# A hybrid encoder layer on one core: order of the input products changed, queries and keys kept as fp16 pairs

## The chip, the cores and the metric

The kernel runs on one core of one Trainium2 chip. The metric is device time in microseconds (us), from three runs: 2857.59 us is the median, 2854.87 to 2858.28 the spread. A kernel is a fixed list of instructions for each engine: TensorE (PE in the profile, with its weight loads, PEld), VectorE (DVE), ScalarE (ACT), GpSimd (POOL) and SyncE (SP), which here only issues transfers. Each engine works through its own list in order and waits, instruction by instruction, for semaphores that the others set.

## What is computed

One encoder layer over 2048 tokens of 1024 features, in fp32. Cut to what matters here:

```python
y = rmsnorm(x, norm_mix_g) @ w_in                  # 1024 -> q 512, k 512, v 512, a 512, g 512
q, k = partial_rotary(q), partial_rotary(k)        # 8 heads of 64; 16 of the 64 dimensions turned
att = dilated_sliding_attention(q, k, v)           # windows (128, 1), (512, 4), (2048, 16)
conv = silu(layernorm(depthwise31(a * sigmoid(g)) + conv_b))
h = x + concat([att, conv]) @ w_out
h = h + cross_attention(rmsnorm(h), rmsnorm(mem))  # 256 memory rows, 4 heads
h = h + square(relu(rmsnorm(h) @ w_up)) @ w_down   # 1024 -> 4096 -> 1024
return rmsnorm(h, norm_final_g)
```

The attention runs over three patterns. A pattern (window, d) looks only at tokens that are a multiple of d apart, within half a window. Each gives an output and a log of its softmax denominator, and the three outputs are combined with the softmax of these logs. For d = 16 the 2048 tokens fall into 16 residue classes of 128 tokens, and one head has 16 score blocks of 128 by 128.

## The kernel before

**Products.** fp32 accuracy is got from pairs: a value is held as a high part and a low part (the value minus the high part), and a product of two pairs is three matmuls into one PSUM accumulation: high by high, high by low, low by high (`mm3`, L254). For the products with `w_in` both factors are fp16 pairs. Weights are first multiplied by a power of two: `wscale` (L189) takes the sum of squares of a weight tile on ACT, adds it over the partitions with a one-column matmul into PSUM bank 7 (kind `c`), and computes the factor `sc` and its inverse `e`, which carries one of the four factors in `back`. `scaled_split` (L210) then scales on ACT, rounds to fp16 on ACT, and subtracts on POOL.

**Stages in time.** First, to 150 us, the memory projections and the preparation of x for tokens 0 to 1023. `xprep(n)` (L379) loads 512 tokens in eight tiles `xn` of 256 KB, normalizes them, transposes them on TensorE (tile `xt`), stores the transposed x to DRAM (`xscr`, needed later as residual) and writes the fp16 pair `xh`, `xl`. Then come the products with `w_in`:

- a gated unit, `glu(c, ns)` (L575), for one of four chunks of 128 channels: products with the weights of g and then of a, each for the groups of 512 tokens in `ns`, tanh on ACT, gate on DVE, store to `uscr`. `early01` is groups 0 and 1. Groups 2 and 3 are done during far attention.
- a unit of queries or keys, `lin_qk(isq, c)` (L691), for the four groups of 512 tokens. c is "r" for the rotary dimensions of all heads (with rotary factors loaded, and sums on DVE and POOL), or 0 to 2 for the others. High and low parts are written by ACT and DVE; they are stored to DRAM, for the near patterns in order of tokens (`qscr`), and by residue class for d = 16 (`qfar` for queries; `kscr` for keys, which all patterns use). In DRAM they are fp32 values (type F32R, for TensorE), the high part rounded to that type.
- the values, `lin_v` (L634): the four column blocks of the weights are scaled by `vmul` (from `vscale`, L607, which uses bank 7 four times), and a first matmul takes x as the stationary factor; 16 tiles `v_0` to `v_15` of 128 tokens, stored to `vtok`.

`pipeline` (L555) takes a list of such units as Python generators and runs them one after another, with later units started ahead by some steps (load, scale, split). `weave` (L93) runs a main generator and calls side generators at given rates; `pinned` (L83) marks each step as not to be issued ahead of the latest instruction noted in `last`. From these calls a list scheduler makes the order of every engine.

Beside the products of queries, keys and values runs the depthwise convolution of tokens 0 to 511 (`conv_units`, tile `cacc`, 31 DVE instructions of 128x512 a chunk): two chunks in the pool `conv0` beside the queries and keys, two in `conv0b` beside gated units and values. Both the units and these pools have their order in the main block:

```python
units = list(chain(glu(0, early01), glu(1, early01)))
units += [lin_qk(isq, c) for c in ("r", 0, 1, 2) for isq in (False, True)]
steps = pipeline(*units, *glu(2, early01), *glu(3, early01), lin_v())
...
    weave(islice(steps, 7), (later, 2.5))
...
    weave(islice(steps, 31), (vsc, 0.42), (conv0, 0.58))
```

`later` is the preparation of x for tokens 1024 to 2047.

**Far attention** (540 to 750 us) is the pattern d = 16 for all heads, together with the near patterns d = 4 and d = 1 of tokens 0 to 511, woven with the gated units of tokens 1024 to 2047 (`rest`). `far_keys` (L928) loads one head's keys `k3` as 16 runs of 144 values in a partition, high parts in partitions 0 to 63, low parts in 64 to 127; `far_q` (L933) loads the queries, the high part twice, the low part once into a tile whose other half is zero. So two matmuls over 128 partitions make one score block: the first gives high by high plus high by low, the second low by high. In `att_far` (L941) four blocks make a unit: each score matmul takes one query block against two neighbouring key blocks at once, 256 columns, of which one half is used; four blocks of 256 columns fill two PSUM tiles `s`. Mask and row minimum on DVE and the exponential on ACT (`att_probs`, L874), four transposes on TensorE to `pt`, the pair `ph` on ACT and `pl` on DVE (`att_turn`, L880), and the products with v (`att_pv`, L891) follow, each a step later. Results go to DRAM (`oscr`) and come back in `combine` (L988) as the tile `ld`.

**Passage and dense part.** From 750 to 796 us far attention ends and the first residual tiles `res` and the attention's output `cath` are loaded. From there to 2867 us the output projection, cross attention and MLP run for each group of 512 tokens (`post`), with near attention of the following groups woven in. There the score matmuls of 256 columns are those of L1097; `load_keys` and `keys_of` (L903, L908) load 16 runs of 64 keys and the queries, and `turned` (L921) reorders queries on POOL.

## Time and profile before

| what | value | how to read it |
|---|---|---|
| median of 3 runs | 2857.59 us | the metric |
| the profiled execution's own time | 2868.5 us | one execution, with the profiler |
| its span | 2866.7 us | first to last instruction, in the trace |
| mean granted clock of TensorE | 0.981 | share of full speed that the throttle allowed |
| DRAM read, written | 389, 160 MB | 192 GB/s over the span |
| depthwise convolution on DVE | 480 instructions, 393.1 us | the largest group of DVE |
| mask and minimum on DVE, exponential on ACT | 384 each, 129.1 and 161.8 us | the largest groups of attention |
| mean of an MLP matmul | 390 to 401 ns | matmuls overlap; two starts are less far apart than this |

The profile says how long each engine was busy in a stretch of time, which granted clock TensorE had there, and ahead of every instruction how long its engine had stood idle and what it waited for (in brackets: the idle time in us, an arrow, the engine or transfer that came last). Idle time matters only on the engine that the others wait for. A matmul's duration in the trace is longer than the step to the next, because matmuls overlap: a price per matmul is read from the distance between two starts. In the stretch of far attention PE was busy 166.8 of 191 us.

### The profile page before, as it was taken

The numbers are of one execution on the slowest core, as the hardware profiler recorded it, in microseconds if no ns is written. First come the engines' busy times: TensorE is split into PE (matmuls) and PEld (weight loads), VectorE is DVE, ScalarE is ACT, GpSimd is POOL, SyncE is SP. The second block draws the span as 40 slices with busy tenths as digits, with TensorE's granted clock in tenths as the row PEclk, the third lists the DMA queues.
The fourth block names the chain that finished last, engine by engine and source line by source line (L and its number), as shares of the span: only waits on it lengthen the run. The fifth ranks groups of instructions, "written<-read, shape, count | busy, mean of one in ns | idle before, by whom it ended". The sixth has DMA issues, their size and how long they took to land.

```text
span 2866.7 us, 40890 instructions
## 1 busy us (share of the span) xinstructions
PE 2744.5 (96%) x14797; PEld 2135.2 (74%) x14797; DVE 1913.0 (67%) x3491; ACT 1277.9 (45%) x2156; POOL 567.1 (20%) x713
## 2 busy tenths in 40 slices
PE   8979999989799999999999999999999999999998
PEld 7844444567587888888888888887888778878877
DVE  5636646355579886568887488766475776667665
ACT  5645331366344433434454534354343544444435
POOL 1236540122201132311221202221020122100000
PEclk9989999999899999999999999999999999999999
DMA  9978864598744766777557867874533564485553
GB/s 266 282 182 213 212 176 134 140 229 220 193 127 131 224 213 213 238 230 219 149 160 227 247 206 226 238 224 158 183 111 122 172 202 162 160 298 160 172 180 103
DMA packets 606787, 551.97 MB, mean 193 GB/s; under 512 B 180965, under 2 KB 481049, under 8 KB 606584
## 3 DMA queue, kind: packets, MB, share of 16 engines
q1 hardware_dynamic: 548296, 462.29, 56.3%
q0 software_dynamic: 20336, 70.17, 6.6%
q10 hardware_dynamic: 37952, 16.88, 2.3%
q8 instruction: 117, 1.92, 0.3%
q14 instruction: 86, 0.70, 0.1%
HBM read 389.18 MB, written 160.06 MB: 192 GB/s over the span
## 4 chain that ended last, share of the span: by engine, by line
PE 69%; DMA 10%; DVE 7%; issue 5%; ACT 5%; POOL 2%; SPq 2%; ACTq 0%; DVEq 0%; POOLq 0%
PE b L1593 6%; PE dn L255 4%; PE dn L256 4%; PE dn L257 4%; PE up L255 4%; PE up L256 3%; PE up L257 3%; PE lin L255 2%; PE lin L256 2%; PE lin L257 2%; SPq L57 2%; PE s L1097 2%; PE pt L884 2%; DMA raw_ub<-in_w_up_dram 2%; PE x L255 1%
## 5 line engine op out<-in xcount | busy, mean ns | idle before, releaser
L272 DVE SCALAR_TENSOR_TENSOR cacc<-cu,cwu,cacc 128x512 f32<-128x512 f32 x480 | 393.1, 820 | 6.4
L878 ACT ACTIVATE sm<-sm,o 128x256 f32<-128x256 f32 (+1 forms) x384 | 161.8, 467 | 118.4 <-DVE o L877 117.8
L255 PE MATMUL dn<-hhh,whi_d 128*128 128x512 f32 x512 | 200.1, 401 | 2.5 <-ACT hhh L1430 1.5
L255 PE MATMUL up<-mh,whi_u 128*128 128x512 f32 x512 | 202.3, 395 | 0.0
L256 PE MATMUL dn<-hhl,whi_d 128*128 128x512 f32 x512 | 200.2, 393 | 0.0
L257 PE MATMUL up<-mh,wlo_u 128*128 128x512 f32 x512 | 200.0, 391 | 0.0
L256 PE MATMUL up<-ml,whi_u 128*128 128x512 f32 x512 | 199.7, 390 | 0.0
L257 PE MATMUL dn<-hhh,wlo_d 128*128 128x512 f32 x512 | 199.6, 393 | 0.0
L877 DVE CUSTOM_DVE_ANT_0 sm<-s,mask 128x256 f32<-128x256 f32 (+1 forms) x384 | 129.1, 375 | 64.4 <-PE s L1097 34.6
L888 DVE TENSOR_TENSOR pl<-pt,ph 128x512 f16<-128x512 f32 x160 | 109.3, 686 | 55.4 <-ACT ph L887 54.7
L233 POOL TENSOR_TENSOR nr<-st_v,mhalf 128x4 f32<-128x4 f32 x12 | 13.3, 1105 | 602.0 <-DVE st_v L229 591.8
L1445 DVE TENSOR_TENSOR h<-h,dn 128x512 f32<-128x512 f32 x128 | 86.4, 683 | 68.2 <-PE dn L257 67.7
L887 ACT CAST ph<-pt 128x512 f16<-128x512 f32 x160 | 92.2, 577 | 79.8 <-PE pt L884 77.8
L884 PE MATMUL pt<-ident,sm 128*128 128x128 f32 x640 | 102.9, 280 | 9.4 <-ACT sm L878 6.2
L257 PEld LDWEIGHTS dn<-hhh,wlo_d 128*128 128x128 f32 x512 | 96.5, 189 | 20.6
L257 PEld LDWEIGHTS up<-mh,wlo_u 128*128 128x128 f32 x512 | 96.1, 188 | 20.5
L255 PEld LDWEIGHTS dn<-hhh,whi_d 128*128 128x128 f32 x512 | 95.5, 188 | 20.6 <-ACT hhh L1430 2.1
L256 PEld LDWEIGHTS dn<-hhl,whi_d 128*128 128x128 f32 x512 | 96.5, 189 | 18.3 <-DVE hhl L1431 0.5
L256 PEld LDWEIGHTS up<-ml,whi_u 128*128 128x128 f32 x512 | 96.3, 188 | 18.6
L255 PEld LDWEIGHTS up<-mh,whi_u 128*128 128x128 f32 x512 | 96.2, 188 | 18.3
L255 PE MATMUL o<-cath,whi_o 128*128 128x512 f32 x256 | 103.4, 405 | 6.4 <-DMA cath<-cath 4.9
L256 PE MATMUL o<-catl,whi_o 128*128 128x512 f32 x256 | 102.8, 401 | 1.7 <-DMA catl<-catl 1.7
(641 smaller groups left out, 8153.8 us busy)
## 6 DMA issues: line engine op xcount, KB each, us to landing
raw_u<-in_w_up_dram SPq DMA_DIRECT2D x64, 512.0 KB
raw_d<-in_w_down_dram SPq DMA_DIRECT2D x64, 512.0 KB
raw_o<-in_w_out_dram SPq DMA_DIRECT2D x32, 512.0 KB
raw_a<-ascr SPq DMA_DIRECT2D x32, 512.0 KB
raw_b<-bscr SPq DMA_DIRECT2D x32, 512.0 KB
lou<-wlo_u POOLq DMA_DIRECT2D x32, 512.0 KB, 5.6
lod<-wlo_d POOLq DMA_DIRECT2D x32, 512.0 KB, 5.4
wlo_u<-lou SPq DMA_DIRECT2D x32, 512.0 KB
```

Source lines behind the costliest of these rows:

```text
L57: (q or nc.sync).dma_start(o, i)
L255: PE.matmul(o, lh, rh, start=first, stop=False)
L256: PE.matmul(o, lh, rl, start=False, stop=False)
L257: last["pe"] = PE.matmul(o, ll, rh, start=False, stop=end)
L272: DVE.scalar_tensor_tensor(acc, u[:, t:t + 512], cwu[:, c, t:t + 1], acc, op0=ALU.mult, op1=ALU.add)
L877: last["dve"] = DVE.tensor_tensor_reduce(dst, so, mask[:, 256 * m:256 * m + nk], 1.0, 3e38, ALU.add, ALU.min, mn)
L878: last["act"] = ACT.activation(dst, dst, AF.Exp, bias=mn, scale=-1.0)
L884: last["pe"] = PE.transpose(pt[:, j, :], sm[:, j, :], ident)
L887: ACT.copy(ph, pt)
L888: DVE.tensor_tensor(pl, pt, ph, op=ALU.subtract)
L1445: last["dve"] = DVE.tensor_tensor(hs[m], hs[m], pt, op=ALU.add)
L1593: PE.matmul(o, w[i][:, k, :], Y[b][q][k], start=first and k + x == 0, stop=k == 3 and x == 2, skip_group_check=not first)
```

## The change

It has five parts.

1. **Order of the units.** All four gated units of groups 0 and 1 come first (sixteen products of 24 matmuls), then keys and queries, then values. Before, two stood ahead of keys and queries and two behind them. The preparation of tokens 1024 to 2047 runs over 15 steps instead of 7, and `xprep` for all groups but the first puts its loads into POOL's queue. One pool holds the convolution's four chunks and the tiles of keys, queries and values, and the rates of the side generators change. `pipeline` starts the second next unit's scaling one step later.
2. **fp16 pairs.** `kscr`, `qscr`, `qfar` and the tiles that feed and read them are fp16. The instructions that round and subtract stay, with fp16 output; the queries' high part gets a tag of its own (`qo`). 
3. **A balance of queries and keys.** `qkscale`, new, loads the query and key columns of `w_in` (16 tiles of 256 KB), squares them on ACT with a sum, adds them over partitions with one matmul and gets a power of two from their ratio. It goes into `back[2]` (queries) and `back[4]` (keys, new), so that both fit fp16 and their product is unchanged.
4. **Keys are read whole**, 16 x 160 fp16 values in one piece a partition, and sliced in SBUF. Far scores are 128 columns each, four blocks in one PSUM tile.
5. **Weight scales.** `wscale`'s square and matmul are marked as not to be issued ahead of the latest TensorE instruction noted.

```diff
-    kscr = dr.tile([2, HD, H, 16, 160], F32R, name="kscr")
-    qscr = dr.tile([2, HD, H, S], F32R, name="qscr")
-    qfar = dr.tile([2, HD, H, 16, P], F32R, name="qfar")
+    kscr = dr.tile([2, HD, H, 16, 160], F16, name="kscr")
+    qscr = dr.tile([2, HD, H, S], F16, name="qscr")
+    qfar = dr.tile([2, HD, H, 16, P], F16, name="qfar")
...
-            ACT.activation(junk, raw, AF.Square, accum_out=v[:, 0:1])
-            yield
-            pc = ps("c", f"sqs_{key}")
-            PE.matmul(pc[:, 0:1], small, v[:, 0:1], start=True, stop=True)
+            with ExitStack() as st:
+                after(st, "pe")
+                ACT.activation(junk, raw, AF.Square, accum_out=v[:, 0:1])
+            yield
+            with ExitStack() as st:
+                after(st, "pe")
+                pc = ps("c", f"sqs_{key}")
+                PE.matmul(pc[:, 0:1], small, v[:, 0:1], start=True, stop=True)
...
-        nat = [load_nat(sp, A["x"][0, 512 * n + P * j:512 * n + P * (j + 1), :], f"xn{n}_{j}") for j in range(4)]
+        nat = [load_nat(sp, A["x"][0, 512 * n + P * j:512 * n + P * (j + 1), :], f"xn{n}_{j}", q=nc.gpsimd if n else None) for j in range(4)]
...
             to(i + 1, 4)
-            to(i + 2, 2)
             to(i + 3, 1)
             for _ in u:
                 yield
-                to(i + 2, 3)
+                to(i + 2, 2)
+            to(i + 2, 3)
...
+    def qkscale():
+
+        acc = top.tile([P, 16], F32, tag="qka", name="qka")
+        for k in range(KC):
+            for x in range(2):
+                t = t2(f"qks{k}{x}")
+                dma(t, w_in[P * k:P * k + P, DATT * x:DATT * x + DATT])
+                with ExitStack() as st:
+                    after(st, "pe")
+                    ACT.activation(t, t, AF.Square, accum_out=acc[:, 8 * x + k:8 * x + k + 1])
+            yield
...
+            PE.matmul(pc[:, 0:2], small, v[:, 0:2], start=True, stop=True)
...
+        pow2_below(v[:, 3:4], v[:, 2:3], v[:, 1:2])
+        DVE.tensor_scalar(back[:, 2:3], back[:, 2:3], v[:, 3:4], None, op0=ALU.mult)
+        DVE.reciprocal(v[:, 0:1], v[:, 3:4])
+        DVE.tensor_scalar(back[:, 4:5], back[:, 0:1], v[:, 0:1], None, op0=ALU.mult)
+        yield
...
-            yield from wscale(raw, nm, 2 if isq else 0)
+            yield from wscale(raw, nm, 2 if isq else 4)
...
-        units = list(chain(glu(0, early01), glu(1, early01)))
+        units = [u for c in range(4) for u in glu(c, early01)]
         units += [lin_qk(isq, c) for c in ("r", 0, 1, 2) for isq in (False, True)]
-        steps = pipeline(*units, *glu(2, early01), *glu(3, early01), lin_v())
+        steps = pipeline(*units, lin_v())
         next(steps)
         later = chain(xprep(sp, 2), xprep(sp, 3))
-        weave(islice(steps, 7), (later, 2.5))
-        drain(later)
+        qks = qkscale()
+        weave(islice(steps, 15), (later, 1.3), (qks, 1))
+        drain(later, qks)
...
-        weave(islice(steps, 31), (vsc, 0.42), (conv0, 0.58))
-        drain(vsc, conv0)
...
+        lbk = lbv = pool("lin_kv", stack=st0)
+        weave(islice(steps, 31), (vsc, 0.6), (conv0, 0.85))
+        drain(vsc)
+        weave(steps, (conv0, 1.5))
+        drain(conv0)
...
-        k = kq.tile([P, 16, 64], F32R, tag="k", name=f"k{p}{h}", bufs=2)
-        dma(f(k), f(kscr[:, :, h].rearrange("x d r i -> (x d) r i")[:, :, 32 * p:32 * p + 64]))
-        return k
+        k = kq.tile([P, 16, 160], F16, tag="k", name=f"k{p}{h}", bufs=2)
+        dma(k, kscr[:, :, h].rearrange("x d r i -> (x d) r i"))
+        return k[:, :, 32 * p:32 * p + 64]
...
-            sg = []
-            for g in range(2):
-                sg.append(ps("S", "s3"))
-                for e in range(2):
-                    z = 2 * g + e
-                    o = sg[g][:, 256 * e:256 * e + 256]
-                    kv = k[:, 4 * rq + 2 * g:4 * rq + 2 * g + 2, PADI:PADI + P]
-                    PE.matmul(o, qh[:, P * z:P * z + P], kv, start=True, stop=False)
-                    last["pe"] = PE.matmul(o, ql[:, P * z:P * z + P], kv, start=False, stop=True)
+            sg = ps("S", "s3")
             for z in range(4):
-                o = sg[z // 2][:, 384 * (z % 2):384 * (z % 2) + P]
-                att_probs(2, 6, o, sm[:, z], os_[:, z, HD + 1:HD + 2])
+                kv = k[:, 4 * rq + z, PADI:PADI + P]
+                PE.matmul(sg[:, P * z:P * z + P], qh[:, P * z:P * z + P], kv, start=True, stop=False)
+                last["pe"] = PE.matmul(sg[:, P * z:P * z + P], ql[:, P * z:P * z + P], kv, start=False, stop=True)
+            for z in range(4):
+                att_probs(2, 6, sg[:, P * z:P * z + P], sm[:, z], os_[:, z, HD + 1:HD + 2])
```

How this moves instructions is shown at three places, by the lists of the engines.

**x into another queue.** SyncE's list before, at the gated units, where tiles `xn` of tokens 512 on stand among stores of gated units (`uscr`) and of transposed x (`xscr`) and the loads of a key weight (`lraw_k`):

```order
L57 DMA xn_2_0_2311<-in_x_dram 128x512
L57 DMA xn_2_1_2312<-in_x_dram 128x512
L57 DMA uscr_70<-u_1_2199 128x512
L57 DMA xscr_78<-xts_4_2207 128x512
L57 DMA xscr_79<-xts_5_2219 128x512
L57 DMA lraw_k_2424<-in_w_in_dram 128x8x48 x2
L57 DMA lraw_k_2424<-in_w_in_dram 128x8x32
L57 DMA xn_3_0_2315<-in_x_dram 128x512
L57 DMA xscr_80<-xts_6_2276 128x512
L57 DMA xn_3_1_2316<-in_x_dram 128x512
```

POOL's list after the change, where they stand among subtractions for the low parts `xl` of x and small powers for scales:

```order
L402 TENSOR_TENSOR xl_1_1686<-xv_5_1886,xh_1_1685 128x512
L57 DMA xn_3_0_2030<-in_x_dram 128x512
L402 TENSOR_TENSOR xl_1_1688<-xv_6_1898,xh_1_1687 128x512
L57 DMA xn_3_1_2031<-in_x_dram 128x512
L57 DMA xn_0_0_2474<-in_x_dram 128x512
L57 DMA xn_0_1_2475<-in_x_dram 128x512
L402 TENSOR_TENSOR xl_1_1688<-xv_7_1910,xh_1_1687 128x512
L237 TENSOR_TENSOR rsx_2051<-st_v,mhalf 128x4
L184 TENSOR_TENSOR sqv_g_1917<-sqv_g_1917,mhalf 128x1
L184 TENSOR_TENSOR sqv_a_1934<-sqv_a_1934,mhalf 128x1
```

The loads of x left SyncE's list; on POOL each stands between instructions of the compute work, and those behind it in the list are issued after it.

**The start of the values.** TensorE's list before, at the end of the gated units that stood there (`lin`, with `lwlo_a3` of the last one), where the first products of the values follow:

```order
L257 LDWEIGHTS lwlo_a30_4262
L257 MATMUL lin_4380<-xh3_1_1687,lwlo_a30_4262 128x512
L255 LDWEIGHTS xh0_0_600
L255 MATMUL v_0_4412<-wvh_4191,xh0_0_600 128x512
L255 LDWEIGHTS xh0_0_600
L255 MATMUL v_1_4442<-wvh_4191,xh0_0_600 128x512
...
L255 MATMUL v_4_4548<-wvh_4191,xh0_1_1681 128x512
L256 LDWEIGHTS xh0_0_600
L256 MATMUL v_0_4412<-wvl_4192,xh0_0_600 128x512
```

The same place after the change, where the products of the last queries (`lwlo_q2`) stand ahead of them:

```order
L261 LDWEIGHTS lwlo_q2_4146
L261 MATMUL lin_4446<-xh3_3_2472,lwlo_q2_4146 128x512
L259 LDWEIGHTS xh0_0_600
L259 MATMUL v_0_4497<-wvh_3928,xh0_0_600 128x512
L260 LDWEIGHTS xh0_0_600
L260 MATMUL v_0_4497<-wvl_3929,xh0_0_600 128x512
L261 LDWEIGHTS xl0_0_601
L261 MATMUL v_0_4497<-wvh_3928,xl0_0_601 128x512
```

Before, five first matmuls of five tiles stood ahead of the first one that needs the low weights `wvl`; now the three matmuls of a product follow one another from the first tile on.

**Far scores.** TensorE's list before, at the first far unit of head 0, between products of a gated unit:

```order
L960 MATMUL s3_5183<-k3_0_5143,qh3_00_5145 128x256
L961 MATMUL s3_5183<-k3_0_5143,ql30_4977 128x256
L960 MATMUL s3_5183<-k3_0_5143,qh3_00_5145 128x256
L961 MATMUL s3_5183<-k3_0_5143,ql30_4977 128x256
L960 MATMUL s3_5188<-k3_0_5143,qh3_00_5145 128x256
L961 MATMUL s3_5188<-k3_0_5143,ql30_4977 128x256
L960 MATMUL s3_5188<-k3_0_5143,qh3_00_5145 128x256
L961 MATMUL s3_5188<-k3_0_5143,ql30_4977 128x256
```

The same unit after the change:

```order
L981 LDWEIGHTS qh3_00_5198
L981 MATMUL s3_5236<-k3_0_5196,qh3_00_5198 128x128
L982 LDWEIGHTS ql30_5030
L982 MATMUL s3_5236<-k3_0_5196,ql30_5030 128x128
L981 LDWEIGHTS qh3_00_5198
L981 MATMUL s3_5236<-k3_0_5196,qh3_00_5198 128x128
L982 LDWEIGHTS ql30_5030
L982 MATMUL s3_5236<-k3_0_5196,ql30_5030 128x128
```

Eight matmuls of 256 columns into two PSUM tiles became eight of 128 columns into one (the last four are not shown), and for fp16 the list shows the weight loads as rows of their own.

72 lines of the change are left out of this document (35 added, 37 removed).

## The prediction

> **What bounds the kernel now.** I read the page first, then the sums by stretch of time, then the gaps in TensorE's timeline. On the page TensorE (PE) is the engine to follow:
>
> ```profile
> PE 2744.5 (96%) x14797; PEld 2135.2 (74%) x14797; DVE 1913.0 (67%) x3491; ACT 1277.9 (45%) x2156; POOL 567.1 (20%) x713
> ```
>
> So time can be won in two ways only: fewer us of matmul, or fewer us in which TensorE stands still or runs at a lower clock. The stretches tell where the second is to be had (columns: stretch, length, busy us of PE, PEld, DVE, ACT, POOL, granted clock, DMA share, GB/s):
>
> ```profile
> 100.00:235.00 135.00, 117.71 (x576) 70.40 (x576) 58.08 (x103) 75.02 (x112) 40.84 (x38) 0.92 0.77 198
> 235.00:425.00 190.00, 188.02 (x894) 87.90 (x893) 109.06 (x166) 74.04 (x93) 104.02 (x95) 1.00 0.86 210
> ...
> 558.00:749.00 191.00, 166.81 (x1579) 133.00 (x1577) 111.89 (x460) 119.40 (x283) 53.00 (x76) 0.95 0.84 207
> 749.00:796.00 47.00, 36.75 (x193) 28.69 (x194) 23.16 (x60) 15.20 (x29) 5.97 (x6) 0.75 0.70 190
> 796.00:2867.00 2071.00, 2027.61 (x10353) 1675.43 (x10351) 1474.46 (x2459) 907.32 (x1467) 324.49 (x454) 0.99 0.61 189
> ```
>
> From 796 us on TensorE is 98% busy at 0.99 of its clock; nearly everything it loses, it loses before. I count a loss as idle time plus (1 - clock) x busy time:
>
> ```profile
> 183.00:214.00 31.00, 21.79 (x95) 11.52 (x94) 16.91 (x31) 15.80 (x24) 12.22 (x12) 0.78 0.60 170
> 426.00:436.00 10.00, 5.88 (x16) 2.07 (x16) 8.41 (x7) 3.98 (x4) 4.75 (x2) 0.66 0.50 137
> 546.00:560.00 14.00, 8.88 (x52) 6.31 (x53) 3.61 (x14) 7.27 (x18) 0.17 (x1) 0.63 0.34 84
> ```
>
> That is 9.2 + 4.8 = 14.0, 4.1 + 2.0 = 6.1 and 5.1 + 3.3 = 8.4 us; far attention (558 to 749) loses 24.2 + 8.3 = 32.5 and the passage to the dense part (749 to 796) 10.3 + 9.2 = 19.4.
>
> **1. Gated units first, x through the POOL queue (183 to 214 us).** What TensorE and SyncE did there:
>
> ```profile
> 188.39 0.48 PE L391 MATMUL xt<-ident,xn 128*128 128x128 f32 x1 [4.40 <-DMA xn<-in_x_dram]
> 208.25 0.61 PE L255 MATMUL lin<-xh,lwhi_kr 128*128 128x512 f16 x1 [3.30 <-ACT lwhi_kr L710]
> ...
> 179.42 5.03 SPq L57 DMA_DIRECT2D lraw_k<-in_w_in_dram  x3
> 184.55 0.65 SPq L57 DMA_DIRECT2D xn<-in_x_dram  x1
> ```
>
> An x tile stood in SyncE's queue behind three loads of a key weight that took until 184.45; its transposes held TensorE 4.4 us. The change puts all 24 loads of tokens 512 on into POOL's queue, and has sixteen products of 24 matmuls (5.2 us each, by 0.21 us a matmul below) to hide the transposes where there were eight. The slow split of the `kr` weights, which cost 3.3 us, gets two such products ahead of it. Added are 16 loads of 256 KB with 16 squares on ACT. At this stretch's 198 GB/s the loads take 21 us, at a DMA share of 0.77 with ACT 75 of 135 us busy; they fit in the 41 us of product that is moved here. If that cover fails, TensorE waits for ACT's weight splits behind these squares. The x loads wait in POOL's queue for free buffers, and queued behind them are the low halves of x and of the weights, which TensorE needs next. Ends: all 14 us back, or 10 lost (two more waits like the 4.4, with their slow clock). I take 11.
>
> **2. Values straight after the queries (426 to 436).**
>
> ```profile
> 428.45 1.77 PE L255 MATMUL v<-wvh,xh 128*128 128x512 f16 x4 [3.65 <-ACT wvh L650]
> ```
>
> TensorE took four first products of values and then had to wait for the low half of the weights. The changed order has whole groups there, with the splits 15 us ahead. The loss of 6.1 goes; ends 0 and 6.1; I take 6.
>
> **3. The start of far attention (546 to 560).**
>
> ```profile
> 522.29 4.66 SPq L57 DMA_DIRECT2D k<-kscr  x1
> 527.00 3.57 SPq L57 DMA_DIRECT2D ql<-qfar  x1
> 530.66 0.53 SPq L57 DMA_DIRECT2D lraw_a<-in_w_in_dram  x1
> ...
> 541.80 0.38 SPq L57 DMA_DIRECT2D lraw_g<-in_w_in_dram  x1
> ...
> 548.63 1.15 ACT L211 ACTIVATE lraw_g<-lraw_g,wscl 128x1024 f32<-128x1024 f32 x1 [6.11 <-DMA lraw_g<-in_w_in_dram]
> ```
>
> Keys and low queries held the queue for 8 us, the two weight loads came late, and the exponentials stood on ACT behind a weight that had not landed. Keys shrink from 1152 to 640 KB and low queries from 256 to 128, but two residual tiles (512 KB) now stand ahead of the weight. The queue's bytes up to it fall by a fifth: 3 to 4 us of its 14. Ends 0 and 8.4; I take 4.
>
> **4. Scores of far attention.** Steps between the starts of neighbours in TensorE's timeline are the price:
>
> ```profile
> 571.16 0.28 PE L961 MATMUL s<-k,ql 128*128 128x256 f32 x1
> 571.28 0.28 PE L960 MATMUL s<-k,qh 128*128 128x256 f32 x1
> ...
> 562.17 0.38 PE L256 MATMUL lin<-xl,lwhi_g 128*128 128x512 f16 x1
> 562.38 0.38 PE L257 MATMUL lin<-xh,lwlo_g 128*128 128x512 f16 x1
> ...
> 559.79 0.40 PE L1097 MATMUL s<-k,qh 128*128 128x256 f32 x1
> 560.02 0.40 PE L1097 MATMUL s<-k,ql 128*128 128x256 f32 x1
> ...
> L960 PE MATMUL s<-k,qh x128: 277/282/775, 540.0 to 739.6; 128*128 128x256 f32 x128
> ```
>
> There are 256 of these (`qh` and `ql`, 128 each), 0.118 us apart, over 256 columns of which 128 are used. In fp16 they take 128 columns. By the 0.2157 us of 512 fp16 columns that is about 0.055; so 256 x 0.063 = 16 us of matmul go. [...] A second, smaller piece: the 64 matmuls whose stationary queries are read with a step of four stand 0.235 us apart; with fp16 steps they could keep that price or fall to 0.11, 0 to 8 us. But this stretch is not bound by TensorE alone:
>
> ```profile
> PE opt L894 <- DVE pl L888: 11.6, 11, 4.1
> ...
> qh<-qfar SPq DMA_DIRECT2D x26, 256.0 KB
> k<-kscr SPq DMA_DIRECT2D x6, 1152.0 KB
> ```
>
> Part of the time saved becomes waiting for the chain scores, exponential, turn, low half. Its waits for `ld` on DVE (behind 13 value loads in SyncE's queue) stay where they are. In return the q and k bytes halve at a DMA share of 0.84, and one PSUM bank a unit instead of two lets the next unit's scores start. Ends 4 and 24; I take 12.
>
> **5. The passage.**
>
> ```profile
> 757.81 8.46 SPq L57 DMA_DIRECT2D res<-xscr  x2
> ...
> 783.98 0.21 PE L892 MATMUL opt<-v,ph 128*128 128x65 f16 x1 [4.15 <-DMA v<-vtok]
> ```
>
> Those residual tiles no longer stand here, so the values behind them come sooner; the load of `cath` that costs 3.7 us stays. Between -5 and 8; I take 3.
>
> **6. Near attention, 384 scores of 256 columns.** 0.118 becomes 0.109 (half of 0.2157 plus 1 ns): 3.5 us, all on TensorE's path. Two waits for queries,
>
> ```profile
> 891.77 0.50 PE L1097 MATMUL s<-k,qh 128*128 128x256 f32 x2 [2.53 <-DMA qh<-qscr]
> 1454.76 0.50 PE L1097 MATMUL s<-k,qh 128*128 128x256 f32 x2 [2.19 <-DMA qh<-qscr]
> ```
>
> move half the bytes; half of them, 2.4, goes. Between 1 and 9; I take 6.
>
> The conversions cost nothing on the path: ACT, DVE and POOL write as many elements as before, beside products that keep TensorE 188 of 190 us busy. Sum: 11 + 6 + 4 + 12 + 3 + 6 = 42 us off the profiled execution, 2868.5 to 2826.5. The median of the runs shown stands at 2857.59 / 2868.5 = 0.9962 of it: **2816 us**.
>
> **Rivals.** *The saved matmul time turns into waiting.* Terms 1 and 4 give nothing: POOL's queue and the squares replace the old waits, and far attention stays with DVE and ACT. For it: 11.6 us of waits for `pl` above, and ACT 63% busy there. Against: TensorE's 167 us of 191. Gain 19, 2839 us.
>
> *TensorE waits behind the convolution on DVE: slower.* Place: the products of keys and queries. The convolution's pieces there rise from 71 to 98 instructions (counted in the order), and sums of squares, value scales and broadcasts all pass through one PSUM bank that DVE must empty:
>
> ```profile
> L272 DVE SCALAR_TENSOR_TENSOR cacc<-cu,cwu,cacc 128x512 f32<-128x512 f32 x63 | 61.3, 973 | 1.2
> ...
> 276.24 0.38 PE L198 MATMUL sqs_k<-sqv_k,small 128*128 128x1 f32 x2 [1.78 <-DVE vs L625]
> ```
>
> DVE's load there is then 98 x 0.973 + 44 of other work = 139 of 166 us (32 products of 5.2), 84%; it was 57%. Sixteen matmuls use that bank; if each waited for one piece of four instructions (3.9 us), 62 us would be lost, net 20: 2878 us. It decides from 42 / 16 = 2.6 us each on. Against: one such wait, 1.78 us, in the trace.
>
> *Short stores.* Keys are stored in pieces of 160 bytes instead of 320. The two hardware queues of the stage:
>
> ```profile
> q1 hardware_dynamic: 64215, 26.50, 54.4%
> q10 hardware_dynamic: 35737, 13.48, 28.9%
> ```
>
> over 195 us and 16 engines give 25 to 26 ns a packet of some 400 bytes. If the 32768 pieces cost 25 ns more, the DMA engines need 0.86 x 190 + 51 = 214 us, the stage grows by 24, and 18 us of the gain stay: 2840 us. [...]
>
> **Chances and numbers.** Forecast 0.70 (alone 2797 to 2838), waiting 0.13, convolution 0.12, short stores 0.05. The lower ends of the six terms add up to 10 us of loss, the upper ones to 69; independent as they are, they will not all fall one way, so the range is 2788 to 2850, which takes in both mild rivals. About 0.2% is what a measurement here can tell from no change. Faster: 0.70 + 0.11 + 0.05 = 0.86; same 0.03; slower 0.11, nearly all of it the convolution.
>
> **What would show it.** Right: no gap over 2 us before `xt`, `lwhi_kr` and the first `v`; far scores under 0.07 us apart and that stretch shorter by 10 us or more. Wrong: gaps before `sqs`, `vss` or `vbc` that end with DVE; POOL waiting on `xn`; `pl` waits that grow as the scores shrink; k stores at 40 ns a packet.

## The result, and the profile after

The changed kernel takes **2887.25 us** (median of 4 runs, 2882.66 to 2891.74), the kernel before 2857.94 us in the same comparison (2854.87 to 2859.93): a ratio of 1.0103, 95% interval 1.0085 to 1.0122. It is slower by 29 us, where 42 us less were forecast. The profiled execution took 2887.18 us, its span is 2885.4 us. That is only 18.7 us more than the span before, since the profiled execution before lay 10 us above its median. Later comparisons ran on chips on which the kernel before took 2868 to 2876 us; so kernels of different comparisons are set side by side by their ratio to it.

The page of the changed kernel hides the loss:

```profile
PE 2742.7 (95%) x14799; PEld 2077.7 (72%) x14799; DVE 1950.6 (68%) x3500; ACT 1305.7 (45%) x2188; POOL 598.8 (21%) x738
```

TensorE is busy 2 us less than before. The stretches of the prediction, for the changed kernel (columns as there):

```profile
100.00:235.00 135.00, 123.29 (x598) 69.94 (x597) 48.28 (x109) 78.58 (x143) 43.50 (x40) 0.95 0.78 212
235.00:425.00 190.00, 155.18 (x697) 70.49 (x695) 139.32 (x159) 83.44 (x82) 116.97 (x84) 0.91 0.53 119
546.00:560.00 14.00, 14.00 (x67) 6.34 (x65) 0.61 (x1) 2.32 (x3) 3.29 (x3) 1.00 0.88 247
558.00:749.00 191.00, 164.71 (x1701) 114.96 (x1699) 116.88 (x497) 127.46 (x305) 54.64 (x77) 0.98 0.62 169
749.00:796.00 47.00, 32.39 (x181) 24.37 (x182) 20.39 (x57) 12.75 (x26) 3.92 (x6) 0.76 0.62 178
796.00:2867.00 2071.00, 2038.64 (x10309) 1645.20 (x10307) 1461.02 (x2451) 898.43 (x1456) 303.07 (x453) 1.00 0.58 186
```

Counted as in the prediction (idle time plus the missing clock), the gated units lose less than before: 11.7 + 6.2 = 17.9 us from 100 to 235, where it was 17.3 + 9.4 = 26.7. The products of keys and queries, where TensorE had been busy 188 of 190 us, now lose 34.8 + 14.0 = 49 us. After 796 us TensorE is idle *less* than before (32.4 us of 2071; it was 43.4) at a clock of 1.00, and yet this part takes longer. Three points of the two traces say how much. For the first two they are the last start in the first row and the first start in the second row (of the tiles `v` and `o`; three numbers for the shortest, median and longest ns, then first and last start), before:

```profile
L256 PE MATMUL v<-wvl,xh x128: 379/379/634, 432.3 to 515.2; 128*128 128x512 f16 x128
...
L255 PE MATMUL o<-cath,whi_o x256: 387/389/796, 750.2 to 2116.5; 128*128 128x512 f32 x128
```

and after the change:

```profile
L260 PE MATMUL v<-wvl,xh x128: 379/379/379, 462.4 to 544.6; 128*128 128x512 f16 x128
...
L259 PE MATMUL o<-cath,whi_o x256: 387/394/796, 752.1 to 2123.3; 128*128 128x512 f32 x128
```

| us | before | after | difference |
|---|---|---|---|
| start to the last product of the values | 515.2 | 544.6 | +29.4 |
| from there to the first output projection (far attention) | 235.0 | 207.5 | -27.5 |
| from there to the end of the span | 2116.5 | 2133.3 | +16.8 |

So two losses stand against one gain. The first loss is one of waits. The changed kernel's waits of TensorE from 235 to 520 us (us in all, times, longest):

```profile
PE sqs_q L202 <- DVE vs L629: 21.9, 2, 16.2
PE lin L259 <- DVE vs L629: 7.5, 1, 7.5
PE vbc L245 <- DVE raw_v L652: 4.8, 2, 2.4
PE vbc L245 <- DVE sqv_q L203: 1.8, 1, 1.8
PE lin L259 <- ACT lwhi_q L216: 1.8, 1, 1.8
```

These are sums and broadcasts that go through PSUM bank 7, as the second rival of the prediction has it. The last loss shows no wait at all. What it shows is the median of the matmuls in the MLP, whose code was not touched. The first row is of the kernel before, the second of the changed one (median 389, then 393 ns):

```profile
L255 PE MATMUL up<-mh,whi_u x512: 387/389/488, 935.8 to 1891.3; 128*128 128x512 f32 x171
```

```profile
L259 PE MATMUL up<-mh,whi_u x512: 387/393/497, 937.2 to 1899.2; 128*128 128x512 f32 x171
```

The steps between the starts of neighbours say the same: of the fp32 matmuls of 512 columns with no wait between them, 77% stood 226 or 227 ns apart before and 27% do now; most of the others take 230 to 238 (worked out from the starts in the traces).

### The profile page after: what moved, and what is told of

It reads as the page before. It is cut to its first block, busy times and chain, and to the rows that moved or that the text cites. A ratio compares the mean times of both kernels' runs of the same rounds, so it can differ in the third digit from the quotient of the medians.

```text
span 2885.4 us, 40956 instructions
## 1 busy us (share of the span) xinstructions
PE 2742.7 (95%) x14799; PEld 2077.7 (72%) x14799; DVE 1950.6 (68%) x3500; ACT 1305.7 (45%) x2188; POOL 598.8 (21%) x738
## 4 chain that ended last, share of the span: by engine, by line
PE 61%; DMA 7%; DVE 5%; ACT 4%; issue 2%; POOL 1%; SPq 1%; ACTq 0%; POOLq 0%; DVEq 0%
PE b L1612 9%; PE dn L259 4%; PE dn L260 4%; PE dn L261 4%; PE up L259 3%; PE up L260 3%; PE up L261 3%; PE x L259 2%; PE x L260 2%; PE x L261 2%; PE xs L259 2%; PE xs L260 2%; PE xs L261 2%; PE pt L909 1%; PE s L1117 1%
## 5 line engine op out<-in xcount | busy, mean ns | idle before, releaser
L276 DVE SCALAR_TENSOR_TENSOR cacc<-cu,cwu,cacc 128x512 f32<-128x512 f32 x480 | 415.8, 869 | 5.8
L902 DVE CUSTOM_DVE_ANT_0 sm<-s,mask 128x256 f32<-128x256 f32 (+1 forms) x384 | 127.1, 374 | 58.4 <-PE s L1117 31.4
L237 POOL TENSOR_TENSOR nr<-st_v,mhalf 128x4 f32<-128x4 f32 x12 | 14.6, 1216 | 614.9 <-DVE st_v L233 614.9
```

What stands on the lines that cost most here:

```text
L276: DVE.scalar_tensor_tensor(acc, u[:, t:t + 512], cwu[:, c, t:t + 1], acc, op0=ALU.mult, op1=ALU.add)
L902: last["dve"] = DVE.tensor_tensor_reduce(dst, so, mask[:, 256 * m:256 * m + nk], 1.0, 3e38, ALU.add, ALU.min, mn)
```

## The experiments

**Where the operands lie: e1, e2, e5, e15.** The change adds two small tiles to the pool `top`: `qka` (64 bytes a partition) and `qkv` (16, for which 32 are set aside). That moves every pool on the right side of SBUF by 96 bytes, among them half of the weights and some moving operands of the dense part. I took the tiles' addresses from the built programs and set them against the steps in the traces.

e1, the changed kernel, back to a multiple of 64 bytes:

```diff
-        v = top.tile([P, 4], F32, tag="qkv", name="qkv")
+        v = top.tile([P, 16], F32, tag="qkv", name="qkv")
```

> The changed kernel with one small tile of the balance (qkv) made 48 bytes larger, so that the pools on the right side of SBUF start at a multiple of 64 bytes again, as before the change; now they start 32 bytes off. Theory A (operands): the fp32 matmuls of 512 columns got slower, median step 0.227 to 0.231 us and more, because in 4440 of 8160 of them the two operands start in different halves of a 64-byte line (medians 232 and 234 ns there, 227 ns where both start in the same half). Then about 2784 x 5 + 1656 x 7 ns = 25 us come back: 2887 to about 2862, and the steps are 0.227 again from 800 us to the end. Theory B (convolution only): the loss is all in the products of keys and queries, where TensorE waited 30 us for DVE: the time stays within 4 us of 2887.

Measured: 2896.43 us, ratio 1.0100 (1.0083 to 1.0116). Nothing came back, and the steps stayed long: theory A fell in the form that I gave it.

e2, the kernel before with the shift alone:

```diff
+    top.tile([P, 24], F32, name="shift")
     lin = ExitStack()
```

> The kernel before with nothing changed but an unused tile of 96 bytes in the pool top, which puts the same 4440 of 8160 matmuls' operands into different halves of a 64-byte line. Theory A: 2858 plus 25 = about 2883, with steps of 0.231 to 0.237 us in the MLP and no new wait. Theory B: 2858 within 4.

Measured: 2899.17 us, ratio 1.0109 (1.0092 to 1.0126), 31 us slower by an unused tile of 96 bytes. So the place matters, though not by halves of 64 bytes; that the hardware has lines of that size was the expectations' assumption, and no run shows it. Sorted by the difference of the two start addresses (moving operand minus weights) modulo 256, the traces agree with each other (worked out from the starts in the traces and the addresses in the programs: number and mean step in ns; matmuls of 512 fp32 columns followed by another one with no wait between):

```
difference modulo 256     before           after            e2               e1
0                         7544  227.7      3382  228.5      3388  228.4      3368  228.3
96                                         2566  233.5      2593  233.5
160                                        1547  233.8      1557  233.9
128                                                                          4115  232.6
192                         56  233.2        64  233.5        54  233.3        64  233.6
```

At each of the four differences other than 0 the mean step is 4.3 to 5.5 ns longer than at 0 in the same run. In e1 the shift had become 128, which is why it brought nothing. Of 8160 such matmuls in the program 4440 have unequal residues after the change: 4440 x 5.1 = 23 us, an estimate over matmuls with no wait between them. (Whether the weights that count are the matmul's own or those being loaded for the next one is not told apart; they mostly have the same residue.)

e5, the shift made 256 bytes in the changed kernel:

```diff
-        v = top.tile([P, 4], F32, tag="qkv", name="qkv")
+        v = top.tile([P, 48], F32, tag="qkv", name="qkv")
```

> The changed kernel with the small tile qkv enlarged to 48 values, so that the pool top is 256 bytes larger than before the change instead of 96, and both operands of nearly all fp32 matmuls start at the same residue modulo 256 bytes, as before. Theory A, corrected (a matmul of 512 fp32 columns takes 5 ns more when moving operand and weights start at different residues modulo 256; in the first alignment they differed by 128): 4440 x 5 ns = 22 us come back, from 29 us above the kernel before to 5 to 10 above it, and the step is 227 ns all through the MLP. Theory D (only the sum of bytes in the pool matters, any enlargement costs): no change, 25 to 33 us above.

Measured: 2873.44 us beside 2871.24, ratio 1.0005 (0.9994 to 1.0015); the changed kernel had 1.0103. From the first output projection to the end it takes 2112.5 us instead of 2133.3, and the row of the MLP is back at 389:

```profile
L259 PE MATMUL up<-mh,whi_u x512: 387/389/504, 938.8 to 1894.8; 128*128 128x512 f32 x171
```

By the ratios 28 us come back, where the expectation had 22. The steps of all 8064 fp32 matmuls of 512 columns from the first output projection on, idle time left out, add up to 1871.6 us before and 1898.9 in e2, and to 1903.7 in the changed kernel and 1876.7 in e5 (worked out from the starts in the traces): 27 us each time, so these matmuls carry nearly all of the difference.

e15, the same 256 bytes in the kernel before:

```diff
+    top.tile([P, 64], F32, name="shift")
     lin = ExitStack()
```

> The kernel before with an unused tile of 256 bytes in the pool top, where e2 had 96. Theory A: all residues modulo 256 are as before, and the time is within 3 us of the kernel before. Theory D (any enlargement costs): about 30 us slower, as e2.

Measured: 2867.63 us beside 2870.92, ratio 0.9997 (0.9982 to 1.0011). It is the residue and not the enlargement: theory A holds in its corrected form, and D falls.

**Why TensorE waits beside keys and queries: e3, e4, e6, e13, e14.** The place is the one that the second rival named; its cause was to be the load of the convolution on DVE. e3 puts the convolution's rate back; e4 is e3 with the edit of e1:

```diff
-        weave(islice(steps, 31), (vsc, 0.6), (conv0, 0.85))
+        weave(islice(steps, 31), (vsc, 0.6), (conv0, 0.58))
```

> The changed kernel with the convolution's old rate (0.58 instead of 0.85 pieces a step) beside keys and queries; the rest of its pieces go beside the values. Theory B: DVE is no longer behind with the reads of the one PSUM bank; TensorE's waits for vs there (30 us) fall under 10 and the time falls by 25 or more, to about 2860. Theory A: the waits fall too, but the far attention, which followed 30 us late and still ended only 2 us late, has less to catch up; the time falls by 5 to 20 and the steps of the MLP stay at 0.231.

> Both edits, alignment and old convolution rate. Theory A: the sum of e1 and e3, 2840 to 2855. Theory B: the same as e3. If what is left of the prediction holds, it is below the kernel before (2858) by 10 or more.

Measured: 2900.32 us, ratio 1.0116 (1.0097 to 1.0134), and 2895.48 us, 1.0098 (1.0082 to 1.0114). Both are misses: no time came back. e3's waits from 235 to 520 us:

```profile
PE sqs_q L202 <- DVE vs L629: 12.3, 1, 12.3
PE lin L259 <- ACT lwhi_q L216: 6.7, 1, 6.7
PE vss L627 <- DVE sqv_k L203: 6.2, 2, 5.9
PE vbc L245 <- DVE raw_v L652: 4.6, 1, 4.6
```

These are the four largest of eight. They changed their names, and all eight still add up to 37 us (39 in the changed kernel). The timeline of DVE in e4 ahead of the longest of them shows why (start, duration, line, operation, idle time before it and what ended it):

```profile
281.86 2.40 DVE L810 SCALAR_TENSOR_TENSOR stl_kr<-rope_kr,wscl,sth_kr 128x512 f16<-128x512 f32 x1 [4.42 <-ACT sth_kr L809]
...
289.88 2.39 DVE L810 SCALAR_TENSOR_TENSOR stl_kr<-rope_kr,wscl,sth_kr 128x512 f16<-128x512 f32 x1 [4.64 <-ACT sth_kr L809]
...
295.08 2.32 DVE L802 SCALAR_TENSOR_TENSOR ql_qr<-rope_qr,wscl,qo_qr 128x512 f16<-128x512 f32 x1 [2.29 <-ACT qo_qr L801]
...
302.83 0.98 DVE L802 SCALAR_TENSOR_TENSOR ql_qr<-rope_qr,wscl,qo_qr 128x512 f16<-128x512 f32 x1 [3.46 <-ACT qo_qr L801]
303.74 0.14 DVE L629 TENSOR_SCALAR vs<-vss 128x1 f32<-128x1 f32 x1
```

No piece of the convolution is ahead of `vs` any more, and DVE is not full. It stands in its own order behind instructions that wait for ACT, and `vs`, which needs 0.14 us and would free the bank, waits behind them. What made this chain long are the writes of the tiles by residue class. The groups of the kernel before from 235 to 470 us (busy us in all, mean ns of one):

```profile
L774 POOL COPY sth_q<-qh_q 128x512 f32<-128x512 f32 x12 | 14.9, 1245 | 17.2 <-issue 10.4 <-ACT qh_q L769 6.8
L777 ACT ACTIVATE sth_k<-lin,wscl 128x512 fp32r<-128x512 f32 x12 | 13.3, 1124 | 8.6 <-issue 6.0 <-DMA kscr<-sth_k 1.4 <-DMA qfar<-stl_q 1.2
L778 DVE SCALAR_TENSOR_TENSOR stl_k<-lin,wscl,sth_k 128x512 fp32r<-128x512 f32 x12 | 13.0, 1096 | 10.7 <-ACT sth_k L777 10.5
```

and of the changed kernel:

```profile
L809 ACT ACTIVATE sth_k<-lin,wscl 128x512 f16<-128x512 f32 x12 | 29.0, 2456 | 8.2 <-PE sqs_q L202 5.7 <-DMA lraw_g<-in_w_in_dram 2.5
L810 DVE SCALAR_TENSOR_TENSOR stl_k<-lin,wscl,sth_k 128x512 f16<-128x512 f32 x12 | 28.8, 2399 | 9.0 <-ACT sth_k L809 5.6 <-DMA qfar<-stl_qr 3.4
L806 POOL COPY sth_q<-qo_q 128x512 f16<-128x512 f16 x10 | 26.2, 2625 | 1.2 <-issue 1.2
```

As many elements, half the bytes, and twice the time on three engines. These instructions take 512 tokens in order and write each to its residue class, so that neighbouring values land 160 bytes apart. e6 writes in the tile's own order (32 contiguous values a class) and reads the source with a step instead:

```diff
-            fh, fl = (t[:, :, sl].rearrange("p r i -> p i r") for t in far)
+            fh, fl = (t[:, :, sl] for t in far)
...
-                    POOL.tensor_copy(ft, t.rearrange("p (i r) -> p i r", r=16))
+                    POOL.tensor_copy(ft, t.rearrange("p (i r) -> p r i", r=16))
...
-                s3 = src.rearrange("p (i r) -> p i r", r=16)
+                s3 = src.rearrange("p (i r) -> p r i", r=16)
```

> The changed kernel with the tiles by residue class written in their own order (16 runs of 32 contiguous fp16 values) and their source read with a step, instead of written with a step of 160 bytes. Theory C (fp16 values written with a step cost ACT, DVE and POOL 2.4 to 2.75 us a tile instead of 1.1 to 1.3, some 85 us over the three engines beside the products of keys and queries, and the chains behind these writes make TensorE wait): the three instructions fall to 0.6 to 1.4 us, the waits for vs and vbc of 30 us fall under 12, the values end 20 us or more earlier, and the time falls by 5 to 25, depending on how much far attention had caught up. Theory B (the convolution's pieces fill DVE): waits and time stay within 4 us. If a read with a step costs what the write did, nothing changes either, but the three instructions stay above 2.3 us.

Measured: 2866.64 us beside 2871.24, ratio 0.9979 (0.9964 to 0.9994): 1.2% under the changed kernel. The groups of e6 (the last one, `qo_q`, reads and writes without a step in both kernels and is there to compare):

```profile
L806 POOL COPY sth_q<-qo_q 128x512 f16<-128x512 f16 x12 | 16.6, 1387 | 4.8 <-issue 3.3 <-ACT qo_q L801 1.5
L810 DVE SCALAR_TENSOR_TENSOR stl_k<-lin,wscl,sth_k 128x512 f16<-128x512 f32 x12 | 9.0, 747 | 13.3 <-ACT sth_k L809 9.2 <-DMA kscr<-stl_k 4.0
L809 ACT ACTIVATE sth_k<-lin,wscl 128x512 f16<-128x512 f32 x12 | 8.0, 678 | 11.4 <-DVE cacc L276 4.8 <-DMA qfar<-sth_q 4.3 <-PE lin L261 2.2
L801 ACT ACTIVATE qo_q<-lin,wscl 128x512 f16<-128x512 f32 x12 | 8.2, 684 | 31.5 <-DMA qscr<-qo_q 13.2 <-POOL stl_q L806 9.9 <-DMA qscr<-ql_q 6.4
```

and its waits from 235 to 520 us, with the row of the values:

```profile
PE sqs_q L202 <- DVE vs L629: 11.9, 2, 8.7
PE sqs_k L202 <- DVE vs L629: 2.2, 1, 2.2
...
L260 PE MATMUL v<-wvl,xh x128: 379/379/380, 428.6 to 510.8; 128*128 128x512 f16 x128
```

With the convolution at its high rate the waits fall from 39 us to 14, the values end at 510.8 us instead of 544.6, and far attention, which now starts early, still takes 210.8 us. Theory C holds, B falls. Two sizes were off: the waits stayed a little above the 12 us that were expected, and the time fell by more than the 5 to 25. The expectation left open that far attention had only caught up with the delay; it had done so by 3 us. Of the 34 us, 29 came through to the end of the profiled execution, and by the ratios the gain is some 35 us.

e13 and e14 ask whether type or step costs it. e13 keeps fp16 and doubles the step to 320 bytes:

```diff
-                far = [lbk.tile([P, 16, 80], F16, tag=f"st{x}", name=f"st{x}_{nm}{hf}", bufs=2)[:, :, 0:w] for x in "hl"]
+                far = [lbk.tile([P, 16, 160], F16, tag=f"st{x}", name=f"st{x}_{nm}{hf}", bufs=2)[:, :, 0:w] for x in "hl"]
```

> The changed kernel with its tiles by residue class twice as wide (160 fp16 values a run, of which 80 are used), so that the step of the writes is 320 bytes, as the fp32 tiles had before. Theory C1 (the type: single 2-byte values cost it): the writes stay at 2.4 to 2.7 us and the time within 5 us of the changed kernel, 29 above the kernel before. Theory C2 (the step: 160 bytes is worse than 320): they fall to 1.1 to 1.3 us, and the time to within 8 us of the kernel before.

e14 makes the swap of e6 in the kernel before:

```diff
-            fh, fl = (t[:, :, sl].rearrange("p r i -> p i r") for t in far)
+            fh, fl = (t[:, :, sl] for t in far)
...
-                s3 = src.rearrange("p (i r) -> p i r", r=16)
+                s3 = src.rearrange("p (i r) -> p r i", r=16)
```

(and the copies on POOL likewise).

> The kernel before with the same swap as in e6: its fp32 tiles by residue class are written contiguously and their source is read with a step. C1: the fp32 writes with a step cost little, so ACT's and DVE's 1.1 us fall to about 0.7, TensorE hardly waited there (98.9% busy), and the time stays within 3 us. C2 or any cost of steps at 4 bytes: the same instructions fall by half and the time by 3 us or more.

Measured: 2901.15 us, ratio 1.0104 (1.0081 to 1.0127), and 2868.63 us, 0.9999 (0.9985 to 1.0014). e13's group and e14's:

```profile
L809 ACT ACTIVATE sth_k<-lin,wscl 128x512 f16<-128x512 f32 x12 | 29.9, 2534 | 8.7 <-PE sqs_q L202 6.3 <-DMA lraw_g<-in_w_in_dram 2.4
```

```profile
L777 ACT ACTIVATE sth_k<-lin,wscl 128x512 fp32r<-128x512 f32 x12 | 8.0, 678 | 8.2 <-issue 6.2 <-DMA qfar<-stl_q 1.4 <-DMA kscr<-sth_k 0.6
```

The type costs it: a step of 320 bytes is no better than one of 160 for fp16 (2534 ns on ACT, where it was 2456), and for fp32 the same step costs 1124 instead of 678. These sources lie in PSUM, where the read with a step cost nothing (678 ns; `qo_q`, without a step, 684). For the rotary dimensions the source lies in SBUF, and there e6 pays for its read (tile `sth_kr`, shortest, median and longest ns):

```profile
L809 ACT ACTIVATE sth_kr<-rope_kr,wscl x4: 1139/1156/1160, 257.1 to 276.1; 128x512 f16<-128x512 f32 x4
```

On ACT a read or a write of fp32 with a step in SBUF takes 1.12 to 1.16 us, where the contiguous one takes 0.68 with its source in PSUM and 0.72 with it in SBUF (`qo_qr`). A write of fp16 with a step takes 2.46 us, so that it costs 1.78 us more than the contiguous one, four times the 0.45 of fp32. Why it is four times as much, no run shows.

**Both mended: e7.** Edits of e5 and e6 together.

> Both edits, alignment to 256 bytes and contiguous writes. Theories A and C together: the sum of e5 and e6, 5 to 25 us under the kernel before; with the prediction's six terms otherwise right, up to 40 under it.

Measured: 2840.85 us beside 2871.24, ratio **0.9895** (0.9878 to 0.9913), 30 us under the kernel before. The two repairs add up within the intervals: 0.0098 + 0.0124 = 0.0222 singly, 0.0208 together.

**What the change itself is worth: e8 to e12,** each from e7. e8 puts far scores back to 256 columns:

```diff
-            sg = ps("S", "s3")
+            sg = []
+            for g in range(2):
+                sg.append(ps("S", "s3"))
+                for e in range(2):
...
+                    kv = k[:, 4 * rq + 2 * g:4 * rq + 2 * g + 2, PADI:PADI + P]
```

> As e7, with the far scores over 256 columns in two PSUM tiles as before the change (fp16 stays): what the halved scores are worth. If far attention is bound by TensorE: 256 matmuls by 0.05 us, 12 us slower than e7. If the chain of scores, exponential, turn and low half bounds it: under 4 us slower, with the waits for pl shrinking as the scores grow.

e9 gives the column sums three banks:

```diff
+    banks["c"] = (7, 3, 4)
     vsc = vscale()
```

> As e7, with three PSUM banks instead of one for the column sums of weight scales and value scales from the products of keys on (the two banks of the transposes of x are free there). e7 still waits 14 us there in three pieces (8.8, 2.0, 3.3) for DVE to empty the one bank. Theory E (the one bank makes the wait: the next sum cannot start): these waits go, and most of 14 us plus 4 us of slow clock with them: 10 to 18 us faster than e7. Theory F (the order of DVE makes it: the factor for the next weights comes late whichever bank it is summed in): the wait moves to the first product that needs these weights; less than 5 us faster.

e10 is both.

> As e9, with the far scores over 256 columns in two PSUM tiles. If the 4 us by which e8 was under e7 are real: 2 to 6 us under e9. If they were the spread of these runs: within 2 us of e9. Against the kernel before: 45 to 50 us under it by theory E, 32 to 38 by F.

e11 takes x back to SyncE's queue:

```diff
-f"xn{n}_{j}", q=nc.gpsimd if n else None) for j in range(4)]
+f"xn{n}_{j}") for j in range(4)]
```

> As e7, with all loads of x in SyncE's queue as before the change: what the move into POOL's queue is worth. The prediction's first term (4.4 us of wait and their slow clock come from x behind weights in SyncE's queue, and the longer stretch of gated units alone does not cure it): 4 to 9 us slower than e7, with a wait of several us for xn again. If sixteen products hide the loads in either queue: within 3 us of e7.

e12 leaves the balance out:

```diff
-        qks = qkscale()
-        weave(islice(steps, 15), (later, 1.3), (qks, 1))
-        drain(later, qks)
+        DVE.tensor_copy(back[:, 4:5], back[:, 0:1])
+        weave(islice(steps, 15), (later, 1.3))
+        drain(later)
     edges()
+    top.tile([P, 16], F32, tag="qka", name="qka")
+    top.tile([P, 48], F32, tag="qkv", name="qkv")
```

(The two small tiles stay, unused, so that the pool `top` keeps its size.)

> As e7, without the balance of queries and keys (16 loads of 256 KB, 16 squares on ACT, one matmul and the small operations behind them are left out; the factor is 1). The prediction costed them at nothing beside the gated units: within 3 us of e7. If they delay the weight splits on ACT (waits of 3.3 us each for lwhi at 167 and 207 us): 4 to 10 us faster.

| | median, us | ratio to before (interval) | last product of values, us | far attention | rest |
|---|---|---|---|---|---|
| e7 | 2840.85 | 0.9895 (0.9878 to 0.9913) | 515.7 | 210.1 | 2111.4 |
| e8 | 2836.75 | 0.9877 (0.9856 to 0.9899) | 512.1 | 211.8 | 2112.6 |
| e9 | 2833.87 | 0.9855 (0.9833 to 0.9877) | 506.2 | 213.3 | 2112.9 |
| e10 | 2827.94 | 0.9831 (0.9808 to 0.9853) | 508.3 | 209.4 | 2110.9 |
| e11 | 2848.26 | 0.9907 (0.9884 to 0.9929) | 524.8 | 211.5 | 2110.1 |
| e12 | 2835.03 | 0.9861 (0.9836 to 0.9886) | 512.3 | 213.0 | 2108.8 |

(e7 and e8 ran in one comparison, the others in another, where the kernel before took 5 us more; the last three columns come from the traces, one execution each, as in the table at the top.)

- e8 is no slower than e7: the halved columns are worth nothing. Their steps do shrink, from a mean of 112 to 62 ns (starts of neighbours), 13 us in all, but in this stretch other things grow: idle time from 24.9 to 30.0, transposes by 2.2, the products with the low half of v by 1.6 us. e9 against e10, in one comparison, says that 128 columns even cost 5.9 us. Far attention of e9 (128 columns), then of e10 (256), in the columns of the stretches:

```profile
506.20:719.50 213.30, 181.93 (x1763) 124.27 (x1761) 117.68 (x498) 131.20 (x309) 58.88 (x80) 0.96 0.64 170
508.30:717.70 209.40, 187.06 (x1763) 130.04 (x1762) 118.03 (x498) 130.82 (x309) 58.88 (x80) 0.99 0.67 173
```

Counted as idle time plus the missing clock, e9 loses 31.4 + 7.3 = 38.7 us there and e10 22.3 + 1.9 = 24.2. So the shorter matmuls were paid for with idle time, and with a granted clock of 0.96 instead of 0.99. Why the clock was lower, no run shows.
- e9: all three waits for `vs` went; what is left from 235 to 520 us is

```profile
PE vss L627 <- POOL vsq L620: 6.1, 1, 6.1
PE lin L261 <- POOL lwlo_q L217: 2.0, 1, 2.0
```

and the values end 9.5 us earlier. Theory E, at its lower end; by the ratios it is 11 us, with intervals that nearly touch. (The span itself is 4.8 us shorter, on a chip on which the kernel before took 5 us more.)
- e11: the wait for `xn` beside the gated units did not come back, but two others did, in the first 100 us, where e7 has 0.3 us of them:

```profile
PE pa L259 <- DMA xn<-in_x_dram: 3.5, 1, 3.5
...
PE xt L395 <- DMA xn<-in_x_dram: 2.8, 1, 2.8
```

The values end 9.1 us later than in e7. By the ratios e11 is 3 us slower, well within the intervals. So the sixteen products cover the loads beside them in either queue; POOL's queue seems to be worth a few us ahead of them, and how many is not settled.
- e12: 3 us faster by the spans of the traces, 10 by ratios whose intervals overlap. TensorE's waits for `lwhi_g` and `lwhi_a` from 100 to 235 us are 7.3 us in e7 and 2.3 in e12; other kernels with the balance have 3.2 (e6) to 5.3 (the changed kernel). What the balance costs, nothing or up to 10 us, is not settled.

e10 is the best version: **1.7% under the kernel before**, 2827.94 us beside 2876.02.

## Why the prediction was wrong, step by step

It failed in two steps: one cost that it declared free, and one that it had no term for.

**"The conversions cost nothing on the path: ACT, DVE and POOL write as many elements as before."** They did write as many, each at 2.4 to 2.75 us instead of 1.1 to 1.4 us. These 64 instructions take some 85 us more over three engines whose queues hold the small operations for weight scales. e6 shows the price to be 1.2%, some 35 us. The second rival had the place (`sqs`, `vss`, `vbc`), the bank and nearly the time (2878 us), and a chance of 0.12, but not the cause: it put it down to the convolution's rate, which e3 refutes. Even so, one bank is part of it: with three, e9 gets another 9.5 us in the trace.

**The sum had no term for the dense part beyond near attention.** That 96 bytes in a pool move half the weights of 2000 us of matmuls was not looked at. The prediction called this part 98% busy and looked for losses only ahead of it, as if the matmuls' own price could not change. e2 shows 31 us for this shift alone, e5 28 us back.

Forecast and result lie 71 us apart. Without the two, e7 is 30 us under the kernel before, where 42 were forecast (0.9895 to the predicted 0.9854), so 59 of the 71 are these two steps and the other 12 lie in the six terms. Term by term, from e7 and its neighbours:

1. *Gated units first, x through POOL (11).* The wait for `xn` went, as forecast; 8.8 us are won from 100 to 235 us in the changed kernel, 5.9 in e7. What cured this wait is the longer cover, not POOL's queue (e11). What the prediction named as the danger came in part: TensorE waits 5.3 us for ACT's weight splits there in the changed kernel and 7.3 in e7, where it had waited 3.3 for `lwhi_kr`.
2. *Values after the queries (6).* Right in e7: no wait over 1 us from the last queries to the end of the values. In the changed kernel `vbc` waited there, another effect of the slow writes.
3. *Start of far attention (4) and* 4. *its scores (12).* The stage is 25 us shorter in e7 (235.0 to 210.1), more than the 16 of both terms. The start is right: in the first 44 us behind the values idle time and missing clock fell from 9.8 to 4.4 us. The scores gave more, but for another reason than the halved columns: with 256 columns in fp16 (e8) the stage is already 23 us shorter. Its scores, with the near ones, took 66 us of steps before, 42 in e8 and 29 in e7. So the kernel with fp16 and 256 columns has 24 us less of them, part of it through the clock (0.94 granted in this stage before, 0.99 in e8). 13 of the 24 are the stage's 120 near scores: 77 of them stood 0.22 us or more apart before, and none does in e8 (median 0.11). That is the smaller piece, where the prediction counted 64 of them and set 0 to 8. Of the 13 us of the halving hardly 2 came through. That is the first rival, true of this part of the term alone. The prediction had the matmul right (0.055 forecast, 0.062 us measured), and its price on the path wrong.
5. *Passage (3) and* 6. *near attention (6).* The rest takes 2111.4 us in e7, 2116.5 before: 5 instead of 9. The near scores in it were under-priced: their steps fell from 54.3 to 40.5 us, 14 where 3.5 were forecast, since most had not stood at 0.118 before (medians 0.117 to 0.136 us by tile); against that, idle time of TensorE grew by 4 us and the fp32 matmuls of 512 columns took 5 more (all from the starts in the traces). In the passage nothing was won: by the windows it loses 14.6 + 7.8 = 22.4 us in the changed kernel, 19.4 before; the wait for `cath` that the prediction named stayed at 3.6 us.

The third rival, short stores, did not happen: the DMA share beside keys and queries fell from 0.86 to 0.53, while TensorE waited. The 32768 packets of 160 bytes took 15 ns each on average, where those of 320 bytes had taken 24; the rival needed 25 ns more a piece, and no run shows that price.

## What to carry to other kernels

A change of type or layout is costed by the pattern of each write, too, and not by its number of elements: if values leave an engine with a step, let the read carry the step, from PSUM where it can (on ACT fp16 took 2.46 us with the step in the write and 0.68 with it in the read from PSUM). After any change to the size of a small tile, compare the median duration of matmuls in code that was not changed; here 5 ns in each of 4440 were worth 28 us, more than any one wait, and a pad of 160 bytes put them right. And when a small operation ends a wait late, look at what its engine itself waits for ahead of it before blaming the engine's load.

## What the runs showed of the hardware that was not expected

- Matmuls of 512 fp32 columns, back to back, stand 227.7 to 228.5 ns apart on average if moving operand and weights start at the same residue modulo 256 bytes, and 232.6 to 233.9 ns if they differ by 96, 128, 160 or 192. fp16 matmuls of 512 columns step at 215 and 216 ns in both kernels, on tiles that moved by 96 bytes and on those that did not; but their operands differ by 64, 96, 160 or 192 in every case, so equal against unequal was not seen for them.
- A 128x512 write of fp16 with each value 160 or 320 bytes from the last takes 2.4 to 2.5 us on ACT and DVE and 2.6 to 2.8 on POOL. Contiguous, with the step in the read instead, it is 0.68 and 0.75 on ACT and DVE from PSUM, 1.4 to 1.5 on POOL from SBUF. A write of fp32 with a step costs 1.12 on ACT, a read of fp32 with a step 1.16 from SBUF and 0.68, as much as a contiguous one, from PSUM.
- The same kernel took 2858 to 2876 us (medians) on the chips of these comparisons, 0.6%.
